# Layer norm of the spatial-gating branch: ordered behind an eviction on ScalarE instead of behind VectorE's last traced instruction

## The chip, the cores and the metric

The kernel runs on one core of a Trainium2 chip. The core has five engines that each work through a queue of their own: TensorE (PE) multiplies matrices, VectorE (DVE) and ScalarE (ACT) work on tiles elementwise, GpSimd (POOL) does simple elementwise work beside them, and SyncE (SP) issues the transfers here. They wait for each other through semaphores. The metric is the device time of one execution in microseconds, as the median of several runs. A profile of one execution shows every instruction with start, duration and the wait ahead of it.

## The reference

One layer of an encoder, on 2048 prompt frames and on 8 x 16 sample frames, with width 1024. What matters here:

```python
h = rmsnorm(x)
u, v, za, q, k, vv, zb, qi, ki, wi, ga, gb = split(h @ w_in)
# mixer A, spatial gating over chunks of 128 frames
u, v = gelu(u), gelu(v)
vn = (v - mean(v)) * rsqrt(var(v) + eps) * ln_g + ln_b          # the layer norm of this case
a = u * (masked sgu_w @ vn + sgu_b) * silu(za)
# mixer B, sparse attention
score = sum over heads of relu(qi . ki) * wi                    # masked by chunk
keep the 256 best keys of each row, softmax attention over them, times silu(zb)
# merge
y = x + (sigmoid(ga) * (a @ w_pa) + sigmoid(gb) * (b @ w_pb)) @ w_out, then rmsnorm
```

The normalised `vn` of the sample frames is an output as well.

## The kernel before

**Tiles and passes.** The frames are 17 tiles of 128 rows: 16 of the prompt and one (number 16) of all sample frames. They are worked on in two halves, `HALVES`: nine tiles (0 to 8) and eight (9 to 16). Projections are made in near-float32 precision with three matmuls each (`mm3`, L173): operands are split into a high part (`split_hi`, ScalarE, L179) and a low part (`split_lo`, L182).

**Phases.** `phase_p1` projects keys, values and queries, for half 0 and then for half 1. `phase_p2` does mixer A and the gates, for half 1 first ("the first pass" below, eight tiles) and then for half 0 ("the second pass", nine tiles). `phase_b` is the attention, tile by tile, with the attention of the sample frames (`attend_sample`, L899 and after) and early merges woven in. `phase_c` merges and projects out.

**Inside phase_p2**, for its tiles: project V in two blocks of 256 columns, evict from PSUM through a gelu on ScalarE into `vn` (L347). VectorE takes mean and variance of each tile (`stats`, L387 and L388), and the reciprocal root for all tiles (`rsqrt`, L186 to L190, into `rs`). Then block b = 0 of U is projected, two tiles to an eviction (L347 into `ug`); while that is traced, the generator `normal` is advanced two steps for each tile, so that the norm of a tile is traced beside U's projection. The norm is two instructions on VectorE in place: L395 subtracts the mean and multiplies by ln_g, L399 multiplies by the reciprocal root and adds ln_b. At its end, in the first pass, one transfer stores the sample tile's rows (L403). Then the first block of ZB is projected (evicted at L352 into "ev", two buffers), then four groups of spatial gating: a matmul of `sgu_w` with `vn` (L430; L435 for the sample tile) into a "tr" bank, and L432 on VectorE that multiplies it into `ug`. Then ZA is projected, evicted through silu into "ev" (L442) and multiplied into `ug` on GpSimd (L444); then the second block of ZB, then `ug` is transposed (L456) and stored; then all of it for block b = 1, and the gates (L472, L506). Projections use four PSUM banks ("mm"), transposes and spatial gating two ("tr"), scores two ("ix").

**The background.** Beside p1 of half 1 and all of p2 runs the selection of the 256 best keys (`select`), as two lanes. A tile's selection first needs scores (L535 and L536 on TensorE, L538 on ScalarE, L540 and L542 on VectorE), then 31 rounds of counting how many scores exceed a candidate (L612 on VectorE and L622 on ScalarE in turn, with small steps L623 to L628), then a mask that is stored (L654 to L663). The lanes take tiles 3, 5, 7, 9, 11, 13, 15 and 2, 4, 6, 8, 10, 16, 12, 14. `weave` mixes both streams into one program by estimated costs at a rate of 0.95.

**What sets the order.** The program order is not the order of the queues. Behind the tracing stands a planner, which plays the program against estimated durations and gives each engine, whenever it is free, the earliest traced instruction whose inputs are ready. An ordering edge without synchronisation makes an instruction stand behind another one in the planner's order; it emits no semaphore. `behind()` lays such an edge from each instruction of the norm to the VectorE instruction that was traced last before it, which by the weaving is often one of the selection.

Of the kernel before, what the change touches and what calls it, by code (L numbers as in the profile page):

```python
# [13 lines left out]
AF = mybir.ActivationFunctionType  # L14
OP = mybir.AluOpType
# [42 lines left out]
def encoder_step(ctx: ExitStack, tc: tile.TileContext, x_prompt, x_sample, cache_k, cache_v, cache_kidx,  # L58
                 norm_g, w_in, ln_g, ln_b, sgu_w, sgu_b, w_pa, w_pb, w_out, final_g,
                 y_prompt, y_sample, o_k, o_v, o_ki, s_k, s_v, s_ki, s_vn):  # L60
    nc = tc.nc
# [255 lines left out]

    AT_FROM = 1

    def behind():  # L320

        return tc.issue_after(next(i for i in reversed(nc.cur_bb.bb.instructions) if i.engine == mybir.EngineType.DVE))

    def phase_p2(half, hT, at_gates=None):

# [7 lines left out]
        def pairs(c, b, use, beside=None, of_beside=1):  # L333
            w = load_w([cols(c + 256 * b)])
            for i in range(0, nt, 2):
# [6 lines left out]
                            next(beside, None)  # L342
                use(pm[:, :m * 256].rearrange("p (j c) -> p j c", j=m), i, m, b * 256)

        def gelu_to(dst, at):
            def use(pm, i, m, c0):
                nc.scalar.activation(dst[:, i:i + m, at:at + 256], pm, AF.Gelu_apprx_tanh)  # L347
            return use

        def gate_b(pm, i, m, c0):  # L350
# [5 lines left out]
        lgb = p2.tile([P, 2, 512], F32, name="lgb")  # L356
# [21 lines left out]
        vn = p2.tile([P, nt, 512], F32, name="vn")  # L378
        st = p2.tile([P, 16, 6], F32, name="st")
        mv = p2.tile([P, 16, 2], F32, name="mv")  # L380
        rs = p2.tile([P, 3, 16], F32, name="rs")
# [9 lines left out]
        def normal():  # L391

            for i in range(nt):
                with behind():
                    nc.vector.scalar_tensor_tensor(vn[:, i], vn[:, i], mv[:, i, 0:1], lgb[:, 0],  # L395
                                                   op0=OP.subtract, op1=OP.mult)
                yield
                with behind():
                    nc.vector.scalar_tensor_tensor(vn[:, i], vn[:, i], rs[:, 1, i:i + 1], lgb[:, 1],  # L399
                                                   op0=OP.mult, op1=OP.add)  # L400
                yield
            if half:
                PS.dma_start(s_vn[0].rearrange("b s c -> (b s) c"), vn[:, nt - 1])  # L403

        beside = stats()
        for b in range(2):
            yield from pairs(C_V, b, gelu_to(vn, b * 256), beside if b else None)
# [3 lines left out]
        nc.vector.tensor_scalar(rs[:, 2, :nt], mv[:, :nt, 1], LN_EPS, None, op0=OP.add)  # L411
        rsqrt(rs[:, 1, :nt], rs[:, 0, :nt], rs[:, 2, :nt])
        beside = normal()
        at_s = {}
        for b in range(2):
            ug = p2.tile([P, nt, 256], F32, tag="ug", name="ug")
            yield from pairs(C_U, b, gelu_to(ug, 0), beside, 2)
            if b == 0:
                for _ in beside:
                    pass  # L420
                yield from pairs(C_ZB, 0, gate_b)
            for g in range(4):
# [3 lines left out]
                for i0 in range(0, np_, 8):  # L426
                    m = min(8, np_ - i0)
                    pm = bank("tr")
# [4 lines left out]
                if half:  # L433
                    pm = bank("tr")
# [14 lines left out]
            for gid, g in zip(gids, gs):  # L449
                i0 = tiles.index(g[0])  # L450
                m = len(g)
# [45 lines left out]
        for r in range(KD):  # L497
            w = load_w([cols(C_GA + P * r, P), w_pa[0][:, P * r:P * (r + 1)]])
            for gid in gids:
# [3 lines left out]
                pm = bank("mm")  # L503
# [609 lines left out]
    def at_gates():  # L1113
        px.append(Pool("p1c", side="right"))
        px.append(Normed(0, px[0], 2).ahead(2))

    back = weave(phase_p2(1, hT, at_gates), back, 0.95)
    hT = px[1].turn()
    px[0].close()
    back = weave(phase_p2(0, hT), back, 0.95)  # L1120
    wp.close()
    hp.close()
# [58 lines left out]
```

## Time and profile before

| | us |
|---|---|
| median of 3 runs | 2271.55 |
| lowest to highest | 2270.2 to 2272.07 |
| the profiled execution | 2267.2 |
| its span, first to last instruction | 2265.4 |
| TensorE busy | 2155.2 (95%) |
| VectorE busy | 1584.4 (70%) |
| ScalarE busy | 1217.8 (54%) |
| GpSimd busy | 592.2 (26%) |
| the norms of the first pass (first start to last start) | 455.5 to 492.1 |
| the norms of the second pass | 1052.8 to 1089.4 |

All times inside the run are microseconds from the start of the span. A row of the stretches gives start and end, length, then for each engine its busy time and how many instructions, then the clock granted to TensorE, the share of the transfer engines that was busy, and GB/s. A row of waits gives who waited for whom: microseconds in total, how often, the longest. A row of the chain of waits gives start, length, engine, and how many instructions in a row. PEld is the weight load of TensorE, which runs beside its matmuls.

### The profile page before, as it was taken

To read this page: it belongs to the slowest core of one execution; us is meant where nothing else is said; L and a number is where in the kernel's file an instruction comes from. 1 tells how busy PE (TensorE), PEld (TensorE's weight loads), DVE (VectorE), ACT (ScalarE), POOL (GpSimd) and SP (SyncE) were. 2 spreads that over 40 slices of the span, in tenths; PEclk is the share of its full clock that TensorE was granted. 3 is DMA by queue.
4 is the path that set the end of the run, shared out by engine and by line. 5 is a ranking of instruction groups with operands and counts; after the bars stand their busy time and mean duration, and the time that the engine had idled before them with its cause. 6 is when DMAs were issued, how large, how long until landed. Compare 5 with 4: busy or idle time off the path is not lost.

```text
span 2265.4 us, 38226 instructions
## 1 busy us (share of the span) xinstructions
PE 2155.2 (95%) x13896; PEld 2027.9 (90%) x13896; DVE 1584.4 (70%) x4057; ACT 1217.8 (54%) x2181; POOL 592.2 (26%) x693
## 2 busy tenths in 40 slices
PE   8999999999999999995799999989999999998998
PEld 7999999999999988993699999978889899987887
DVE  7105867897787797748996787577867689855442
ACT  6225546646665655435655654277756667753221
POOL 1221222232432231210125222123253423334100
PEclk9999999999999999995799999989999999999999
DMA  6233233122432233111115222454344431044342
GB/s 206 80 108 113 80 98 98 56 78 80 133 99 86 84 92 112 49 56 28 36 44 152 68 78 85 114 145 116 93 137 125 123 102 38 15 144 150 130 154 79
DMA packets 251005, 218.83 MB, mean 97 GB/s; under 512 B 46528, under 2 KB 238656, under 8 KB 250816
## 3 DMA queue, kind: packets, MB, share of 16 engines
q1 hardware_dynamic: 250816, 216.39, 32.3%
q8 instruction: 109, 1.79, 0.3%
q14 instruction: 80, 0.66, 0.1%
HBM read 152.45 MB, written 63.81 MB: 95 GB/s over the span
## 4 chain that ended last, share of the span: by engine, by line
PE 79%; DVE 7%; DMA 6%; ACT 3%; issue 2%; POOL 2%; SPq 1%; ACTq 0%; POOLq 0%; DVEq 0%
PE ps_mm L173 54%; PE ps_po L778 5%; PE ps_tr L761 4%; PE ps_ix L535 2%; PE ps_ix L536 2%; PE ps_mm L737 2%; PE ps_mm L738 2%; PE ps_ix L173 2%; DVE junk L612 2%; DMA ws<-in_w_in_dram 1%; PE ps_mm L789 1%; DMA qi<-qi_s 1%; DMA q<-q_s 1%; PE ps_tr L252 1%; POOL wl L182 1%
## 5 line engine op out<-in xcount | busy, mean ns | idle before, releaser
L182 POOL TENSOR_TENSOR wl<-ws,wh 128x256 fp32r<-128x256 f32 (+1 forms) x376 | 306.2, 844 | 930.1 <-ACT wh L179 895.3
L173 PE MATMUL ps_mm<-wh,hh 128*128 128x256 f32 (+1 forms) x1360 | 395.7, 292 | 5.7 <-ACT hh L179 3.5
L622 ACT ACTIVATE junk<-s,bc 128x384 int8<-128x384 f32 (+14 forms) x232 | 294.1, 1268 | 196.7 <-DVE bc L628 195.4
L173 PE MATMUL ps_mm<-wh,hl 128*128 128x256 f32 (+1 forms) x1360 | 395.3, 291 | 0.9 <-DVE hl L182 0.9
L173 PE MATMUL ps_mm<-wl,hh 128*128 128x256 f32 (+1 forms) x1360 | 393.9, 290 | 0.2 <-POOL wl L182 0.2
L173 PE MATMUL ps_mm<-hh,wh 128*128 128x384 f32 (+1 forms) x1152 | 378.2, 328 | 0.0
L173 PE MATMUL ps_mm<-hl,wh 128*128 128x384 f32 (+1 forms) x1152 | 377.7, 328 | 0.0
L173 PE MATMUL ps_mm<-hh,wl 128*128 128x384 f32 (+1 forms) x1152 | 376.8, 328 | 0.0
L612 DVE TENSOR_SCALAR_CACHE_REDUCE junk<-s,bc 128x512 int8<-128x512 f32 (+14 forms) x248 | 351.7, 1421 | 5.0
L173 PEld LDWEIGHTS ps_mm<-wh,hh 128*128 128x128 f32 x1360 | 262.2, 193 | 11.6 <-ACT hh L179 4.7
L173 PEld LDWEIGHTS ps_mm<-wh,hl 128*128 128x128 f32 x1360 | 262.2, 193 | 4.0 <-DVE hl L182 1.2
L173 PEld LDWEIGHTS ps_mm<-wl,hh 128*128 128x128 f32 x1360 | 262.3, 193 | 3.3 <-issue 1.2
L542 DVE SCALAR_TENSOR_TENSOR s<-r,wiw,s 128x384 f32<-128x384 f32 (+2 forms) x266 | 201.7, 780 | 65.3 <-ACT r L538 64.7
L173 PEld LDWEIGHTS ps_mm<-hh,wh 128*128 128x128 f32 x1152 | 217.1, 188 | 2.2
L173 PEld LDWEIGHTS ps_mm<-hl,wh 128*128 128x128 f32 x1152 | 217.1, 189 | 1.6
L173 PEld LDWEIGHTS ps_mm<-hh,wl 128*128 128x128 f32 x1152 | 217.0, 188 | 1.8
L538 ACT ACTIVATE r<-ps_ix 128x512 f32<-128x512 f32 (+2 forms) x304 | 156.7, 538 | 100.0 <-PE ps_ix L536 89.9
L761 PE MATMUL ps_tr<-ident,sx 128*128 128x128 f32 x1088 | 169.6, 275 | 5.3 <-DVE ptl L182 4.2
L182 DVE TENSOR_TENSOR ptl<-ps_tr,pth 128x512 fp32r<-128x512 f32 (+1 forms) x231 | 149.9, 659 | 28.4 <-ACT pth L179 27.2
L744 ACT ACTIVATE sx<-sx,mx 128x128 f32<-128x128 f32 (+15 forms) x128 | 153.7, 1202 | 29.0 <-DVE mx L743 28.5
L179 ACT ACTIVATE pth<-ps_tr 128x512 fp32r<-128x512 f32 (+1 forms) x231 | 126.9, 572 | 64.9 <-PE ps_tr L761 57.3
L778 PE MATMUL ps_po<-pth,vst 128*128 128x256 f32 x544 | 157.1, 306 | 3.3 <-ACT pth L179 1.8
(287 smaller groups left out, 4578.5 us busy)
## 6 DMA issues: line engine op xcount, KB each, us to landing
ws<-in_w_in_dram SPq DMA_DIRECT2D x88, 512.0 KB, 3.9
x<-in_x_prompt_dram SPq DMA_DIRECT2D x41, 512.0 KB, 3.6
q<-q_s SPq DMA_DIRECT2D x34, 256.0 KB, 4.1
out_dram<-x SPq DMA_DIRECT2D x17, 512.0 KB, 2.6
gb_s<-ev SPq DMA_DIRECT2D x40, 192.0 KB, 2.3
ma_s<-ev SPq DMA_DIRECT2D x40, 192.0 KB, 1.9
ma<-ma_s SPq DMA_DIRECT2D x40, 192.0 KB, 3.1
sg<-gb_s SPq DMA_DIRECT2D x40, 192.0 KB, 2.5
```

The source lines that it names most:

```text
L173: nc.tensor.matmul(out, a(k), b(k), start=(n == 0), stop=(n == 3 * nk - 1))
L179: nc.scalar.activation(dst, src, AF.Copy)
L182: (eng or nc.vector).tensor_tensor(dst, src, hi.bitcast(F32), op=OP.subtract)
L535: nc.tensor.matmul(pi[:, :n], hi[:, h, :], kist[:, c:c + n], start=True, stop=False)
L536: nc.tensor.matmul(pi[:, :n], lo[:, h, :], kist[:, c:c + n], start=False, stop=True)
L538: nc.scalar.activation(r[:, :n], pi[:, :n], AF.Relu, scale=HD ** -0.5)
L542: nc.vector.scalar_tensor_tensor(s[:, c:c + n], r[:, :n], wiw[:, t, h:h + 1], s[:, c:c + n], op0=OP.mult, op1=OP.add)
L612: nc.vector.tensor_scalar(junk[:, :L], s[:, :L], thr, 0.0, op0=op, op1=OP.add, accum_out=cnt)
L622: nc.scalar.activation(junk[:, :L], s[:, :L], AF.Sign, bias=candf, scale=-1.0, accum_out=cnt)
L744: nc.scalar.activation(sx, sx, AF.Exp, bias=mx[:, 7:8], scale=HD ** -0.5, accum_out=T.rsum[:, h:h + 1])
L761: nc.tensor.transpose(tv[:, l, hh * P:(hh + 1) * P], pr[hh][:, (l0 + l) * P:(l0 + l + 1) * P], ident)
L778: nc.tensor.matmul(po, vst[:, l0 + l, n, :], pp[:, l, :], start=(l0 + l == 0 and i == 0), stop=(l0 + l == t and i == 1))
```

## The change

`behind()` goes away. In its place `issue_behind(ins, before)` lays one ordering edge without synchronisation from an instruction to another one, also of another engine. The gelu eviction of V and U keeps its instruction in `evicted[0]`. The first step of a tile's norm (L395) is laid behind the gelu eviction that was traced last, so behind V's last one for tiles 0 and 1 of the pass, behind U's first for tiles 2 and 3, and so on, two tiles to an eviction. The second step (L399) has no ordering edge any more; it needs the first by its data.

```diff
-    def behind():
-
-        return tc.issue_after(next(i for i in reversed(nc.cur_bb.bb.instructions) if i.engine == mybir.EngineType.DVE))
+    def issue_behind(ins, before):
+
+        tc.add_manual_dep(ins.ins, before.ins.name,
+                          mybir.DependencyInfo(mybir.DependencyClass.NoSync, mybir.DependencyReason.DATA),
+                          reason="issue_behind")
...
+        evicted = [None]
+
         def gelu_to(dst, at):
             def use(pm, i, m, c0):
-                nc.scalar.activation(dst[:, i:i + m, at:at + 256], pm, AF.Gelu_apprx_tanh)
+                evicted[0] = nc.scalar.activation(dst[:, i:i + m, at:at + 256], pm, AF.Gelu_apprx_tanh)
             return use
...
             for i in range(nt):
-                with behind():
-                    nc.vector.scalar_tensor_tensor(vn[:, i], vn[:, i], mv[:, i, 0:1], lgb[:, 0],
-                                                   op0=OP.subtract, op1=OP.mult)
+                issue_behind(nc.vector.scalar_tensor_tensor(vn[:, i], vn[:, i], mv[:, i, 0:1], lgb[:, 0],
+                                                            op0=OP.subtract, op1=OP.mult), evicted[0])
                 yield
-                with behind():
-                    nc.vector.scalar_tensor_tensor(vn[:, i], vn[:, i], rs[:, 1, i:i + 1], lgb[:, 1],
-                                                   op0=OP.mult, op1=OP.add)
+                nc.vector.scalar_tensor_tensor(vn[:, i], vn[:, i], rs[:, 1, i:i + 1], lgb[:, 1],
+                                               op0=OP.mult, op1=OP.add)
                 yield
```

## The prediction

> **What bounds the kernel now.** I read the page first: the forty slices and the chain of waits.
>
> ```profile
> PE   8999999999999999995799999989999999998998
> ...
> PEclk9999999999999999995799999989999999999999
> ...
> PE 79%; DVE 7%; DMA 6%; ACT 3%; issue 2%; POOL 2%; SPq 1%; ACTq 0%; POOLq 0%; DVEq 0%
> ```
>
> TensorE sets the time nearly everywhere. The exception is slices 19 and 20 of 40 (56.6 us each, so 1019 to 1133 us), where PE falls to 5 and 7 tenths and its clock with it. Idle and slow PE time there is what can be won. Next, busy time by stretch: the hole, the stretch behind it, the start of the attention phase.
>
> ```profile
> core 0: us, PE busy (x) PEld busy (x) DVE busy (x) ACT busy (x) POOL busy (x), PEclk, DMA share, GB/s
> 930.00:955.00 25.00, 25.00 (x211) 25.00 (x210) 14.24 (x62) 12.24 (x26) 5.65 (x8) 1.00 0.17 49
> 1017.00:1103.00 86.00, 45.61 (x102) 24.05 (x101) 74.72 (x153) 44.77 (x67) 6.87 (x9) 0.56 0.09 24
> 1103.00:1465.00 362.00, 361.72 (x2213) 354.85 (x2213) 276.57 (x529) 194.42 (x282) 101.63 (x123) 0.99 0.29 85
> 1465.00:1505.00 40.00, 32.27 (x160) 26.22 (x161) 25.86 (x107) 27.66 (x83) 8.59 (x9) 0.74 0.69 169
> ```
>
> In 1017 to 1103, PE is idle 40.4 of 86 us and runs at a clock of 0.56; in the 362 us after, it is never idle. So whatever fills the hole moves all of 1103 to 1465 forward. Then, who waits for whom in the hole: first PE's waits, then all engines'.
>
> ```profile
> PE ps_tr L430 <- DVE vn L399: 17.0, 2, 15.0
> PE ps_ix L535 <- ACT qih L179: 11.7, 2, 5.9
> ...
> POOL ug L444 <- DVE bg L627: 75.8, 1, 75.8
> ```
>
> The spatial-gating matmuls (L430) wait for the second layer-norm step (L399). That looks like 17 us, but GpSimd's L444 has stood still 75.8 us: it multiplies the gate into ug, which L432 fills from L430's output. While it stands, by the code, the two "ev" buffers and then the "mm" banks stay taken, and no projection can be evicted. What PE does in the hole is scores for the background selection, and their small waits (L535) fill time in which PE has nothing else. The root is the norms' lateness. The two steps' busy time by stretch (L395; L399's row for the last stretch is the same), and the evictions of U and of the ZB projection after it (first and last start):
>
> ```profile
> 455.00:493.00 38.00, 5.98 (x8) 1.00 0.28 77
> 925.00:1050.00 125.00, 0.00 (x0) 0.91 0.17 50
> 1050.00:1092.00 42.00, 6.68 (x9) 0.50 0.05 13
> ...
> L347 ACT ACTIVATE ug<-ps_mm x5: 383/598/599, 931.3 to 950.4; 128x512 f32<-128x512 f32 x4, 128x256 f32<-128x256 f32 x1
> ...
> L352 ACT ACTIVATE ev<-ps_mm x5: 385/597/600, 956.8 to 977.0; 128x512 f32<-128x512 f32 x4, 128x256 f32<-128x256 f32 x1
> ```
>
> In the second pass the nine tiles are normalised between 1050 and 1092, though U's evictions were over at 951. The timeline of VectorE shows what they are queued behind:
>
> ```profile
> 932.10 0.17 DVE L190 TENSOR_TENSOR rs<-rs 128x9 f32<-128x9 f32 x1
> ...
> 1060.86 2.08 DVE L612 TENSOR_SCALAR_CACHE_REDUCE junk<-s,bc 128x1792 int8<-128x1792 f32 x1
> ...
> 1062.86 0.75 DVE L395 SCALAR_TENSOR_TENSOR vn<-vn,mv,lgb 128x512 f32<-128x512 f32 x1
> 1063.53 0.74 DVE L542 SCALAR_TENSOR_TENSOR s<-r,wiw,s 128x512 f32<-128x512 f32 x1
> ...
> 1086.13 2.08 PE L430 MATMUL ps_tr<-vn,wst 128*128 128x512 f32 x2 [15.00 <-DVE vn L399]
> ```
>
> Their last input (rs, L190) is complete at 932.3; they stand behind counts and scores of the selections of tiles 13 and 12 (1792 and 1664 columns), the work traced before them. The selection runs over 100 us behind its place in the program, and the edge carries that lag into the norms.
>
> **The change part by part.** It removes 34 ordering edges (17 tiles, two steps) on VectorE, and adds 17, from each first step to an eviction on ScalarE; a second step follows its first by its data alone. No instruction is added or dropped, and the new edge is order only, without a wait. If one were emitted after all, the evictions it names in the second pass lie at or before 947.5 (U's last but one), before or among the norms' possible places, and VectorE idles 10.8 of 25 us in 930 to 955; behind such a wait stand only selection steps, on which no projection depends. I take 0.
>
> *Second pass, the norms.* 18 instructions at 0.74 us (6.68 + 6.68 = 13.4 us in all) need that idle time: 10.8 us to 955 and the rest soon after, so vn is complete near 960 to 965, before the ZB projection, the next in the program, is through (its last eviction is at 977). L430 then runs without a wait.
>
> *The hole.* What PE must still do in 1017.5 to 1102.7 (85.2 us), by form, and the same at full clock from the chain of waits elsewhere:
>
> ```profile
> L535 PE MATMUL ps_ix<-kist,qih 128*128 128x384 f32 x26 | 14.8, 570 | 6.9 <-ACT r L538 6.6
> L536 PE MATMUL ps_ix<-kist,qi 128*128 128x384 f32 x26 | 12.8, 494 | 0.0
> L430 PE MATMUL ps_tr<-vn,wst 128*128 128x512 f32 x8 | 8.2, 1135 | 15.5 <-DVE vn L399 15.0 <-DVE ug L432 0.5
> L535 PE MATMUL ps_ix<-kist,qih 128*128 128x512 f32 x11 | 7.6, 709 | 14.1 <-ACT qih L179 11.7 <-ACT r L538 2.4
> L536 PE MATMUL ps_ix<-kist,qi 128*128 128x512 f32 x11 | 6.6, 616 | 0.2
> ...
> 974.11 0.23 PE ps_ix L535
> ...
> 1152.69 1.03 PE ps_tr L430 x4
> ...
> 1157.37 0.86 PE ps_tr L430 x2
> 1188.69 0.66 PE ps_tr L456 x6
> ```
>
> 22 score matmuls of 512 columns at 0.235 us are 5.2; 52 of 384 at three quarters of that, 9.2; eight large L430 at 0.43 are 3.4, eight small at (1.03 - 0.86) / 2 = 0.085 are 0.7; L456 with two projection matmuls, 0.9. Sum 19.4 us. The hole is worth at most 85.2 - 19.4 = **65.8 us**: the last gate matmul, now at 1465, would end near 1399.
>
> *What is late next.* The selection. Its last mask piece and, on the chain, PE's first step after the gates:
>
> ```profile
> L661 DVE SCALAR_TENSOR_TENSOR pen<-junk,eq x4: 550/687/692, 1442.6 to 1453.0; 128x512 bf16<-128x512 int8 x3, 128x384 bf16<-128x384 int8 x1
> ...
> 1465.20 0.44 PE ps_ix L899 x2
> ...
> 1400.00:1440.00 40.00, 40.00 (x231) 40.00 (x230) 25.94 (x54) 16.00 (x21) 8.53 (x12) 1.00 0.20 64
> ```
>
> It ends at 1453.0 + 0.55 = 1453.6, 12 us before the gates. VectorE is 87% busy in the hole (74.72 of 86), so the selection is paced by it there. Taking the norms' 13.4 us out brings its end to about 1440. Between 1399 and 1440 PE has the attention phase to start on. The selection leaves VectorE free for 35% (25.94 of 40 busy), and the attention phase used 65% of it (25.86 of 40), so I let it go at 0.35 / 0.65 = 54% of its pace: 41 x 0.54 = 22 us. Gain: 1465 - 1440 = 25, and 22 more, **47 us**. Bounds: nothing of the attention phase before the selection ends gives 25, no contention 66. I take 47, since the VectorE rows price the overlap.
>
> *Clock.* Two stretches of 10 us, columns as above. A PE 81% busy stayed at 0.50; at 100% it came back.
>
> ```profile
> 1050.00:1060.00 10.00, 8.08 (x18) 4.99 (x19) 9.93 (x20) 6.29 (x12) 0.00 (x0) 0.50 0.00 0
> 1110.00:1120.00 10.00, 10.00 (x87) 10.00 (x86) 9.62 (x25) 8.43 (x11) 0.00 (x0) 1.00 0.16 54
> ```
>
> In 1399 to 1440 PE would be 54% of 81% busy (32.27 of 40), so perhaps at half clock; its work there at full clock is 41 x 0.44 = 18 us, 36 at half, and still fits. So the sum stands. [...]
>
> *First pass.* The eight norms stand at 455 to 493, the U evictions are over at 441, so they move forward by some 35 us. PE was 37.4 of 40 us busy in the stretch of L430:
>
> ```profile
> L347 ACT ACTIVATE ug<-ps_mm x4: 592/597/599, 420.9 to 440.7; 128x512 f32<-128x512 f32 x4
> ...
> 480.00:520.00 40.00, 37.40 (x266) 34.86 (x265) 38.00 (x101) 18.45 (x34) 14.37 (x17) 0.91 0.21 66
> L403 SPq DMA_DIRECT2D out_dram<-vn x1: 357/357/357, 492.8 to 492.8; - x1
> ```
>
> At most 2.6 us of idle and 0.09 x 40 = 3.6 of clock come back; a loss of the same size is as possible, if norms displace selection steps on a VectorE that is 38 of 40 busy. I take 0 of -6 to +6. The one transfer moved is the store of the last tile (L403). It goes forward with the norms on SyncE's queue; a load behind it can only start earlier.
>
> *Sum.* The profiled execution took 2267.2 us, its span 2265.4. 2267.2 - 47 = 2220. The median of the runs, 2271.55, is 4.35 above the profiled one, so the forecast is **2224**. Its own range, 25 to 66 won and the first pass's 6 halved either way: 2202 to 2250.
>
> **Rivals.**
>
> *The selection gates everything behind it.* On PE, the first step behind the gates is L899 of the sample attention, which needs the selection's memory and came 11.6 us after the mask (1465.2). If the planner leaves L899 ahead of the attention phase in PE's queue, PE waits until 1440 + 12 = 1452: gain 13, **2258**. For it: that is today's order. Against: the tiles of the attention phase do not need that memory, and a planner that orders by readiness will see PE free.
>
> *Slower: the scores are thinned out.* In the hole PE gave the scores of tile 12 a pair every 1.4 us; where projections compete for PE, tiles 15 and 14 got one every 2.6.
>
> ```profile
> L535 PE MATMUL ps_ix<-kist,qih x62: 332/390/796, 1159.8 to 1321.4; 128*128 128x512 f32 x54, 128*128 128x384 f32 x8
> ...
> L535 PE MATMUL ps_ix<-kist,qih x37: 393/558/797, 1017.6 to 1069.2; 128*128 128x384 f32 x26, 128*128 128x512 f32 x11
> ```
>
> (161.6 / 62 and 51.6 / 37.) A filled hole makes the 32 pairs of tile 12 take 32 x 1.2 = 38 us more. If nothing of that is won back and L899 still stands first, PE restarts at 1453.6 + 38 + 11.6 = 1503: 38 us lost, **2310**. It decides once the mask's end comes after 1453.6. Against: the other lane counts faster meanwhile, and tiles 15 and 14 are scored only after it.
>
> *The change does not do what it says.* The planner still puts older VectorE work first, the norms stay at 1050: **2271**. Against: VectorE idled 43% of 930 to 955, with no older work ready.
>
> **Chances.** Forecast 0.59, PE held by the selection 0.20, no effect 0.08, slower 0.10, more than 66 won 0.03. A measurement here tells 0.2% (4.5 us) from no change. Faster: 0.59 + 0.20 + 0.03 = 0.82; same 0.08; slower 0.10. The range takes the forecast and the first rival: 2200 to 2264.
>
> **What would show it.** L395 and L399 of the second pass at 932 to 970; no wait of L430 for vn and none of L444 over 10 us; slices 19 and 20 of PE and clock at 9; the last gate matmul near 1400; the last L661 near 1440; attention matmuls (L737) before it. Wrong, if the norms are early and the hole stays (then something other than vn holds "ev"), or if PE idles as long just before L899.

## The result and the profile after

| | before | after |
|---|---|---|
| median of 4 runs each, same chip, us | 2270.88 | 2242.09 |
| lowest to highest | 2269.09 to 2272.07 | 2231.59 to 2244.56 |
| the profiled execution | 2267.2 | 2242.49 |

The ratio is 0.9865, with a 95% interval of 0.9833 to 0.9897: the changed kernel is faster by 28.8 us in the medians, 24.7 between the two profiled executions. The forecast was 2224, with 47 us gained. The hole was filled as forecast, all 66 us of it, but 41 us were given back in the attention phase.

The page after, its totals and three of the lines of its forty slices:

```profile
span 2240.7 us, 38226 instructions
...
PE 2144.5 (96%) x13896; PEld 2030.0 (91%) x13896; DVE 1588.7 (71%) x4057; ACT 1215.8 (54%) x2181; POOL 594.8 (27%) x693
...
PE   8999999999999999999999999588999999998998
...
DVE  7105857988897797856787678899788677755443
...
PEclk9999999999999999999999999699999999999999
```

The dip of PE and of its clock has left slices 19 and 20. A new one stands in slices 26 to 28 (a slice is now 56.0 us, so 1400 to 1568), where PE is at 5, 8 and 8 tenths and the clock at 6 in the first. It is shallower and longer. VectorE (DVE) is at 8, 9 and 9 there.

Line numbers have moved by two or three: the norm's steps are L398 and L401 (were L395 and L399), counting is L614 (was L612), the last step of a score L544 (was L542), a mask piece L663 (was L661), the gates L508 (was L506), attention logits L739 (was L737), the sample attention L901 (was L899). The norms of the second pass, the end of the gates, the last mask and the start of the attention, by source line:

```profile
L398 DVE SCALAR_TENSOR_TENSOR vn<-vn,mv,lgb x9: 717/745/1159, 919.0 to 943.8; 128x512 f32<-128x512 f32 x9
L401 DVE SCALAR_TENSOR_TENSOR vn<-vn,rs,lgb x9: 741/752/1229, 928.8 to 944.6; 128x512 f32<-128x512 f32 x9
L508 DVE TENSOR_TENSOR ev<-ev,ps_mm x15: 529/550/555, 1305.0 to 1398.8; 128x384 f32<-128x384 f32 x15
L663 DVE SCALAR_TENSOR_TENSOR pen<-junk,eq x8: 556/683/693, 1390.0 to 1555.6; 128x512 bf16<-128x512 int8 x7, 128x384 bf16<-128x384 int8 x1
L739 PE MATMUL ps_mm<-kst,qh x320: 280/403/668, 1411.2 to 1968.9; 128*128 128x512 f32 x92, 128*128 128x384 f32 x60, 128*128 128x128 f32 x4, 128*128 128x256 f32 x4
L901 PE MATMUL ps_ix<-ident,kc x32: 270/272/421, 1568.1 to 1713.7; 128*128 128x128 f32 x32
```

The same lines of the kernel before, where the prediction did not show them:

```profile
L506 DVE TENSOR_TENSOR ev<-ev,ps_mm x24: 528/550/555, 1320.5 to 1464.4; 128x384 f32<-128x384 f32 x24
L737 PE MATMUL ps_mm<-kst,qh x320: 278/396/776, 1475.9 to 1993.5; 128*128 128x512 f32 x92, 128*128 128x384 f32 x60, 128*128 128x128 f32 x4, 128*128 128x256 f32 x4
```

The norms are through at 945 (before: 1090). The last gate starts at 1398.8 instead of 1464.4, the attention at 1411.2 instead of 1475.9: both 65 us earlier. But the last mask piece starts at 1555.6, 103 us later than the 1453.0 of before, and the last attention logit is only 25 us earlier (1968.9 against 1993.5).

Where the 41 us went is read from the stretches, first of after (the old hole, the overlap of selection and attention in two cuts, the rest, the whole attention phase), then of before (the first 157 us of its attention phase and all of it). The columns are those of the prediction's stretches.

```profile
1017.00:1103.00 86.00, 85.26 (x649) 82.00 (x648) 61.16 (x112) 53.43 (x86) 19.12 (x22) 1.00 0.22 64
...
1399.00:1440.00 41.00, 21.76 (x93) 17.94 (x94) 32.19 (x106) 27.47 (x66) 7.74 (x8) 0.58 0.53 124
1399.00:1556.00 157.00, 115.89 (x706) 102.98 (x707) 140.31 (x422) 111.42 (x248) 42.80 (x43) 0.83 0.35 87
1556.00:1985.00 429.00, 421.90 (x2936) 389.70 (x2935) 329.65 (x926) 292.31 (x518) 149.56 (x160) 0.99 0.36 97
1399.00:1985.00 586.00, 537.80 (x3639) 492.69 (x3640) 469.96 (x1347) 403.74 (x765) 192.35 (x203) 0.94 0.35 95
```

```profile
1465.00:1622.00 157.00, 143.83 (x944) 125.99 (x944) 120.46 (x429) 120.05 (x302) 42.74 (x48) 0.93 0.46 118
1465.00:2010.00 545.00, 521.69 (x3636) 480.83 (x3636) 420.86 (x1246) 385.70 (x745) 186.36 (x194) 0.97 0.35 97
```

The old hole holds 85.26 us of PE work in 86, at full clock. The attention phase, with the same work (3639 matmuls in the trace, 3636 before), takes 586 us instead of 545. Of these 41 us, 25 are PE idle (586 - 537.8 = 48.2 against 545 - 521.7 = 23.3) and 16 are the same work at a lower clock (537.8 against 521.7 busy, clock 0.94 against 0.97). Both lie in the first 157 us, up to the end of the last mask: 706 matmuls are done there instead of 944. VectorE is 89% busy in it (140.31) against 77% (120.46). Counting alone (L614) is 27 us of that, in this row of the same stretch with only that line's instructions:

```profile
1399.00:1556.00 157.00, 26.59 (x24) 0.83 0.35 87
```

Gain and loss add up: 66 - 41 = 25, the difference of the profiled executions.

Why is the selection 103 us late? Tile 14 is the last one of its lane, behind tile 12. The scores of tile 12, by the accumulating step on VectorE of 28 of its 32 pairs, before and after:

```profile
L542 DVE SCALAR_TENSOR_TENSOR s<-r,wiw,s x28: 607/612/751, 1033.3 to 1066.6; 128x384 f32<-128x384 f32 x21, 128x512 f32<-128x512 f32 x7
```

```profile
L544 DVE SCALAR_TENSOR_TENSOR s<-r,wiw,s x28: 603/620/1257, 1049.5 to 1102.6; 128x384 f32<-128x384 f32 x21, 128x512 f32<-128x512 f32 x7
```

In the hole they took 33 us, among projections 53, and they end 36 us later. The counting of tile 14 follows, its first and last count on VectorE, before and after:

```profile
L612 DVE TENSOR_SCALAR_CACHE_REDUCE junk<-s x1: 2153/2153/2153, 1323.3 to 1323.3; 128x1920 int8<-128x1920 f32 x1
...
L612 DVE TENSOR_SCALAR_CACHE_REDUCE junk<-s,bc x24: 2187/2212/2347, 1303.0 to 1437.4; 128x1920 int8<-128x1920 f32 x17, 128x2048 int8<-128x2048 f32 x7
```

```profile
L614 DVE TENSOR_SCALAR_CACHE_REDUCE junk<-s x1: 2153/2153/2153, 1351.0 to 1351.0; 128x1920 int8<-128x1920 f32 x1
...
L614 DVE TENSOR_SCALAR_CACHE_REDUCE junk<-s,bc x23: 2197/2212/2347, 1339.7 to 1512.7; 128x1920 int8<-128x1920 f32 x17, 128x2048 int8<-128x2048 f32 x6
```

It starts 28 us late (1351.0 against 1323.3), takes 162 us instead of 114, and its last mask piece starts 43 us after the last count instead of 16: 28 + 48 + 27 gives the 103. Before, this tail lay under the gates, and the two together left VectorE 35% free (25.94 of 40 us busy from 1400 to 1440); now most of it (1399 to 1556) lies under the attention, which kept VectorE 77% busy without it (120.46 of 157 in the kernel before). The tail also holds up a part of the attention: `attend_sample` begins by freeing the memory of the selection, and its first matmul (L901) starts at 1568.1, 12.5 us after the last mask piece; with the tail shortened, in the second run below, it starts at 1479.1, 14 us after that run's last piece. Of the 238 matmuls that are missing in the first 157 us, 147 are those of the sample attention (before, 147 stand in 1465 to 1622; after, none in 1399 to 1556), and 91 are those of the tiles (797 before, 706 after).

### The profile page after: what moved, and what is told of

Its sections match the earlier page's. It is cut to its first block, busy times and chain, and to the rows that moved or that the text cites. A ratio compares the mean times of both kernels' runs of the same rounds, so it can differ in the third digit from the quotient of the medians.

```text
span 2240.7 us, 38226 instructions
## 1 busy us (share of the span) xinstructions
PE 2144.5 (96%) x13896; PEld 2030.0 (91%) x13896; DVE 1588.7 (71%) x4057; ACT 1215.8 (54%) x2181; POOL 594.8 (27%) x693
## 5 line engine op out<-in xcount | busy, mean ns | idle before, releaser
L182 POOL TENSOR_TENSOR wl<-ws,wh 128x256 fp32r<-128x256 f32 (+1 forms) x376 | 310.7, 856 | 915.7 <-ACT wh L179 903.7
L614 DVE TENSOR_SCALAR_CACHE_REDUCE junk<-s,bc 128x512 int8<-128x512 f32 (+14 forms) x248 | 351.9, 1421 | 5.2
L544 DVE SCALAR_TENSOR_TENSOR s<-r,wiw,s 128x384 f32<-128x384 f32 (+2 forms) x266 | 201.5, 774 | 65.0 <-ACT r L540 64.2
L763 PE MATMUL ps_tr<-ident,sx 128*128 128x128 f32 x1088 | 177.0, 281 | 14.8 <-ACT sx L746 4.3
L780 PE MATMUL ps_po<-pth,vst 128*128 128x256 f32 x544 | 161.7, 313 | 9.3 <-ACT osb L784 8.8
L182 DVE TENSOR_TENSOR ptl<-ps_tr,pth 128x512 fp32r<-128x512 f32 (+1 forms) x231 | 149.6, 658 | 28.7 <-ACT pth L179 27.7
```

The source lines that it names most:

```text
L182: (eng or nc.vector).tensor_tensor(dst, src, hi.bitcast(F32), op=OP.subtract)
L544: nc.vector.scalar_tensor_tensor(s[:, c:c + n], r[:, :n], wiw[:, t, h:h + 1], s[:, c:c + n], op0=OP.mult, op1=OP.add)
L614: nc.vector.tensor_scalar(junk[:, :L], s[:, :L], thr, 0.0, op0=op, op1=OP.add, accum_out=cnt)
L763: nc.tensor.transpose(tv[:, l, hh * P:(hh + 1) * P], pr[hh][:, (l0 + l) * P:(l0 + l + 1) * P], ident)
L780: nc.tensor.matmul(po, vst[:, l0 + l, n, :], pp[:, l, :], start=(l0 + l == 0 and i == 0), stop=(l0 + l == t and i == 1))
```

## The experiments

All were timed against the kernel before on the same chip. Its median was 2268.11 to 2270.01 in these sets, against 2270.88 in the table above, so distances between kernels of different sets can be off by up to 3 us. Two theories were tested first, called A and B in what was expected. By A, the 41 us are the price of the selection's tail sharing VectorE with the attention. By B, the attention phase loses them whether the tail is there or not.

**The tail shortened, without and with the change.** In both kernels tile 14 counts 10 of its 31 rounds; the other 21 are left out, so its threshold is coarse.

```diff
-        for b in range(30, -1, -1):
+        for b in range(30, 20 if t == 14 else -1, -1):
```

> The kernel before, where the selection of tile 14, the last to finish, counts 10 of its 31 rounds; 21 rounds are left out, so its mask is not exact. Control for the next run. Theory A (66 us were won before the gates' end, and 41 of them are given back because the selection's tail runs into the attention phase on VectorE): here the tail ends before the gates anyway, so the time hardly moves, 2262 to 2271 us, gates still end near 1465. Theory B (the attention phase has a slow start of its own whenever it begins, for its loads and the half clock): the same, 2262 to 2271.

> The changed kernel with the same 21 rounds of tile 14 left out. Theory A: the selection ends near 1400, the gates near 1399, so the whole 66 us stays: 2200 to 2212 us, 55 us or more under the run above, PE idle and half clock behind the gates as in the kernel before (attention phase 545 us long). Theory B: the start stays slow, 2230 to 2242 us, 28 us under the run above, attention phase 586 us long.

Measured: 2266.56 on the kernel before (ratio 0.9984, 0.9973 to 0.9996), 2219.99 on the changed one (0.9774, 0.9752 to 0.9796). The tail is worth almost nothing before and 22 us after, so it is part of the give-back; but 2220 lies between the two theories. VectorE's timeline of the shortened changed kernel shows that the tail had not gone:

```profile
1404.26 0.74 DVE L661 SCALAR_TENSOR_TENSOR eq<-pre,bd,eq 128x512 f32<-128x512 f32 x1
...
1457.25 1.28 DVE L657 TENSOR_TENSOR_SCAN pre<-eq,bl 128x512 f32<-128x512 f32 x1
1458.56 0.67 DVE L741 CUSTOM_DVE_ANT_0 sx<-ps_mm,pen 128x512 f32<-128x512 f32 x1
1460.17 0.69 DVE L182 TENSOR_TENSOR ptl<-ps_tr,pth 128x512 fp32r<-128x512 f32 x1 [0.86 <-ACT pth L179]
...
1464.65 0.68 DVE L663 SCALAR_TENSOR_TENSOR pen<-junk,eq 128x512 bf16<-128x512 int8 x1
```

Masks (L657, L661, L663) still run among attention steps (L741 and the split L182) until 1465. So the test was made again with the tail gone.

**The tail taken away.** Tile 15 counts 10 rounds and tile 14 four; 48 rounds of the two are left out.

```diff
-        for b in range(30, -1, -1):
+        for b in range(30, {14: 26, 15: 20}.get(t, -1), -1):
```

> The kernel before with 10 rounds of tile 15 and 4 of tile 14 (the other 48 rounds left out): the selection ends near 1370, well before the gates, which stay near 1465. Both theories: 2255 to 2268 us. Control for the next run.

> The changed kernel with the same rounds left out, so that the masks too are done before 1400 (in the earlier run with 10 rounds of tile 14 two masks, 8 pieces, still ran to 1465 in the attention phase, and 47 of 66 us were kept). Theory A, the tail of the selection on VectorE is the whole of what is given back: 60 to 67 us under the run above. Theory B, part of the loss belongs to the attention phase itself: the distance stays at 45 to 52 us.

Measured: 2264.25 before (0.9981, 0.9968 to 0.9993) and 2200.15 after (0.97, 0.9684 to 0.9716). Without the tail the change is worth 64.1 us, the size of the hole. Masks and attention of the changed kernel without the tail:

```profile
L663 DVE SCALAR_TENSOR_TENSOR pen<-junk,eq x12: 283/692/1225, 1221.0 to 1383.0; 128x512 bf16<-128x512 int8 x10, 128x128 bf16<-128x128 int8 x1, 128x384 bf16<-128x384 int8 x1
...
1396.00:1553.00 157.00, 144.07 (x945) 125.82 (x945) 120.64 (x430) 119.63 (x302) 41.57 (x48) 0.95 0.47 117
1396.00:1941.00 545.00, 522.22 (x3634) 480.05 (x3634) 420.81 (x1247) 385.56 (x745) 185.46 (x194) 0.98 0.35 97
...
L901 PE MATMUL ps_ix<-ident,kc x32: 270/273/435, 1395.6 to 1536.7; 128*128 128x128 f32 x32
```

The last mask starts before the attention does, and the attention phase is the old one again, 545 us with 522 us of PE work. B falls, and of A it is shown that the tail is the whole of what is given back. How the tail costs that is not shown: without it VectorE is less busy (120.64 of 157 us), but the sample attention also starts with the attention phase again (L901 at 1395.6), and this test does not separate the two, nor VectorE's time from ScalarE's or from that of small transfers. PE's longest waits in the overlap of the changed kernel (1399 to 1556) name no single engine either:

```profile
PE ps_tr L699 <- DMA kk<-out_dram: 11.5, 2, 7.1
PE ps_po L780 <- ACT osb L784: 7.7, 5, 2.6
PE ps_mm L739 <- DVE mx L741: 6.2, 3, 3.6
```

**VectorE relieved in the overlap.** One of five splits of the attention's probabilities goes over GpSimd; here three of five for the tiles 0 to 5.

```diff
-            if turn[0] % POOL_OF in POOL_TURNS:
+            if turn[0] % POOL_OF in (POOL_TURNS if t > 5 else (0, 2, 4)):
```

> The changed kernel, where for attention tiles 0 to 5 three of five splits of the probabilities go to GpSimd instead of one of five: some 19 splits of 0.66 us, 12 us, leave VectorE in the stretch where it is busy 152.6 of 170 us (1390 to 1560). Theory A (VectorE bounds that stretch): 4 to 12 us faster than the changed kernel, 2230 to 2238 us, and the selection's last mask earlier than 1556. Rival (latency and ScalarE, which gets one more copy a split, bound it): 2242 us or more.

Measured: 2231.01 (0.9836, 0.9817 to 0.9855), 11 us under the full change by the medians; the two intervals overlap (0.9833 to 0.9897 for the full change), so the gain is not clear of the spread. The overlap:

```profile
1399.00:1556.00 157.00, 121.87 (x735) 106.48 (x736) 138.21 (x424) 116.78 (x260) 80.91 (x91) 0.83 0.45 113
...
L663 DVE SCALAR_TENSOR_TENSOR pen<-junk,eq x6: 540/690/1110, 1399.9 to 1526.1; 128x512 bf16<-128x512 int8 x5, 128x384 bf16<-128x384 int8 x1
```

GpSimd takes 38 us more, the last mask starts 30 us earlier (1526.1), and PE does 6 us more in the stretch, where it is still 35 us idle. So VectorE's load holds the tail up. How much it holds the attention up is not shown: of the 29 matmuls more, 19 are those of the sample attention, which starts earlier too (1537.5), and up to 1526, with the tail in both kernels, 552 are done against 537.

**The second pass alone.** The old edges stay in the first pass.

```diff
...
+            if half:
+                for i in range(nt):
+                    with behind():
...
+            else:
+                for i in range(nt):
+                    issue_behind(...)
...
```

> The new edge in the second pass alone, the old edges in the first. Theory A and B: all of the gain comes from the hole of the second pass: 2239 to 2246 us, the same as the full change within 4 us. Rival C (the first pass has a share, by moving the later order): over 2250 or under 2235 us.

Measured: 2239.71 (0.9874, 0.9851 to 0.9897), as the full change. The norms by pass:

```profile
L404 DVE SCALAR_TENSOR_TENSOR vn<-vn,mv,lgb x8: 743/747/748, 453.4 to 488.5; 128x512 f32<-128x512 f32 x8
...
L413 DVE SCALAR_TENSOR_TENSOR vn<-vn,mv,lgb x9: 734/743/750, 921.7 to 946.2; 128x512 f32<-128x512 f32 x9
```

The first pass keeps its old places (453 to 489) and nothing is missing: the gain comes from the second pass.

**No ordering edge at all.**

```diff
-                issue_behind(nc.vector.scalar_tensor_tensor(...), evicted[0])
+                nc.vector.scalar_tensor_tensor(...)
```

> The changed kernel without the new edge: the norms have no ordering edge at all. Theory: what helps is that the old edge is gone, the evictions named by the new one are over before a norm's turn comes; 2238 to 2247 us, the norms of the second pass at 915 to 950 as in the changed kernel. Rival (the new edge holds the norms back from displacing statistics or selection steps): over 2250 us.

Measured: 2228.65 (0.9825, 0.9804 to 0.9846), 13 us under the changed kernel by the medians and outside what was expected; the ends of the two intervals overlap. Norms, and a stretch of the second pass without the edge, then that stretch with it:

```profile
L398 DVE SCALAR_TENSOR_TENSOR vn<-vn,mv,lgb x9: 714/747/1294, 897.7 to 922.3; 128x512 f32<-128x512 f32 x9
...
1110.00:1200.00 90.00, 89.36 (x508) 87.89 (x507) 74.98 (x150) 59.99 (x94) 34.25 (x40) 1.00 0.41 128
```

```profile
1110.00:1200.00 90.00, 87.09 (x488) 85.33 (x487) 73.51 (x151) 60.24 (x93) 33.75 (x37) 0.98 0.38 117
```

The norms start 21 us earlier still (897.7 against 919.0), so the new edge does hold them back, against the theory. PE idles 2 us less in this stretch, and the gates end about 10 us earlier. A single wait that went away was not found; the whole order changes a little. What this gain is stays open; in the last run below it does not show.

**A third bank for the scores.** The selection is late because tile 12's scores are slow. By the prediction that was TensorE's share; a score also waits for one of two banks to be evicted (before, from 1010 to 1110, the score matmuls L535 waited ten times for the eviction L538, 8.9 us in all). One bank of the projections is given to it, on the changed kernel and on the kernel before.

```diff
-    bank.set(mm=4, tr=2, ix=2)
+    bank.set(mm=3, tr=2, ix=3)
```

> The changed kernel with three PSUM banks for scores and three for projections, instead of two and four. Theory (scores are thinned out because a pair waits for a bank while projections take PE in turn): the scores of tile 12 take under 55 us instead of some 62 (1043 to 1105), tile 14's counting starts before 1340 instead of 1351, and the time is 2228 to 2240 us. Rival (three banks hold the projections up as much): 2242 to 2260 us.

> The kernel before, with its old edges, and three PSUM banks for scores and three for projections. The old edge holds a norm until the selection reaches the place traced ahead of it; with three banks tile 13 was counted from 956 instead of 1029 us in the changed kernel, so the selection's lag shrinks by some 73 us. Theory (the hole is the selection's lag, carried into the norms by the old edge): the norms come near 980 to 1015, the hole shrinks from 85 us to 15 or less, 2205 to 2225 us. Rival (the hole belongs to the edge whatever the lag): the hole stays, 2240 us or more, only the tail is freed.

Measured: 2202.43 on the changed kernel (0.9708, 0.9693 to 0.9722), far below what was expected, and the fastest kernel of this study that leaves no rounds out, 40 us under the changed one and 68 under the one before. On the kernel before, 2210.66 (0.9743, 0.9724 to 0.9761), 57 us won by the banks alone. The changed kernel with three banks: its scores of tile 12, its last mask and gates, and its stretches.

```profile
L544 DVE SCALAR_TENSOR_TENSOR s<-r,wiw,s x28: 603/614/1220, 967.7 to 1001.3; 128x384 f32<-128x384 f32 x21, 128x512 f32<-128x512 f32 x7
...
L663 DVE SCALAR_TENSOR_TENSOR pen<-junk,eq x8: 559/692/1111, 1280.9 to 1350.7; 128x512 bf16<-128x512 int8 x7, 128x384 bf16<-128x384 int8 x1
L508 DVE TENSOR_TENSOR ev<-ev,ps_mm x17: 542/553/556, 1303.3 to 1401.1; 128x384 f32<-128x384 f32 x17
...
960.00:1060.00 100.00, 100.00 (x785) 97.31 (x784) 87.54 (x192) 72.35 (x104) 25.05 (x33) 1.00 0.20 60
1402.00:1559.00 157.00, 146.00 (x931) 126.25 (x931) 118.63 (x424) 117.95 (x297) 40.18 (x46) 0.91 0.45 115
```

With PE 100% busy the 28 pairs take 33.6 us, as long as with two banks and an idle PE (33.3). The last mask starts at 1350.7, before the gates end, and the overlap is gone: PE does 146.00 us of work in the first 157 us of the attention, as before the change (143.83). The gates end 2 us later (1401.6 against 1399.3), so the projections lose little that shows. The edit also takes a bank from the projections, and the 28 pairs now stand some 80 us earlier; which of these makes the pairs faster was not tested apart. The kernel before with three banks, its norms and the same stretch:

```profile
L395 DVE SCALAR_TENSOR_TENSOR vn<-vn,mv,lgb x9: 740/745/1320, 989.5 to 1026.0; 128x512 f32<-128x512 f32 x9
...
960.00:1060.00 100.00, 94.40 (x698) 89.52 (x697) 86.80 (x180) 66.37 (x94) 24.01 (x33) 0.95 0.17 51
```

The old edges stand, but the selection that they carry runs ahead, so the norms come at 990 and only 5.6 us of PE are left idle. The hole was the old edge times the selection's lag; with three banks the change of this case is worth 8 us (2210.66 against 2202.43).

**No edge, three banks.** Both edits together.

> The norms without any ordering edge, and three score banks: the two versions that were fastest by themselves (2228.65 and 2202.43 us). If what the missing edge won (13 us) is its own: 2188 to 2196 us. If it was won only against the selection's lag, which the third bank has taken away: 2198 to 2207 us.

Measured: 2207.25 (0.9726, 0.9702 to 0.9751), not better than 2202.43. What the missing edge won with two banks, if it was clear of the spread, is not its own.

## Why the prediction was right or wrong

*What bounds the kernel, and the root of the hole: right.* With the norms early, the spatial gating's wait for vn has gone. PE's longest wait from 900 to 1399 after the change:

```profile
PE ps_mm L173 <- ACT ev L474: 2.4, 1, 2.4
```

GpSimd's multiply (now L446) did wait 14.8 us once, where the prediction had none over 10; it was for ScalarE, not for vn, and PE did not stand behind it, as its longest wait, 2.4 us, shows. GpSimd's row in the same stretch:

```profile
POOL ug L446 <- ACT r L540: 14.8, 1, 14.8
```

*The norms of the second pass: right* (919 to 945, predicted 932 to 970). What the new edge costs is not settled: without any edge the norms start 21 us earlier and the median is 13 us lower, but with three banks it is not lower.

*The hole: right.* 65.8 us at most were worked out, 65 to 66 measured. *First pass: right*, 0 of -6 to +6: the first norm moved forward by 43 us (412.5 from 455.5; some 35 forecast), and the second pass alone gives the same time.

*What is late next: this step failed.* "Taking the norms' 13.4 us out brings its end to about 1440." It came to 1556, later than before instead of earlier. The step kept the pace that the selection has while PE is empty, and took only VectorE's relief into account. But the hole was also what fed it: in it the scores had PE to themselves. The prediction saw this in its slower rival, with 38 us for tile 12, and put the 38 us into that rival alone, where they belonged in the sum of the forecast as well. (Measured: 36 us later, 20 of them by slower scores, 53 against 33 us for 28 pairs, and 16 by a later start, so the good agreement is partly luck.) Only 28 of the 103 us were there when the counting of tile 14 began. The other 75 came while the tail ran beside the gates and the attention; the forecast let the attention go slower beside the selection, but not the selection beside the attention.

*The pace of the overlap: near in the stretch that was priced, but not its cause.* The 54% was taken for 41 us. From 1399 to 1440, 93 matmuls were done, about as many as the kernel before did in its first 25 us of attention:

```profile
1465.00:1490.00 25.00, 20.38 (x88) 16.04 (x89) 13.37 (x65) 14.63 (x43) 2.47 (x3) 0.66 0.80 199
```

By this count some 15 us were lost there, with 41 - 22 = 19 forecast. But the overlap lasted 157 us, and over all of it the attention lost 41, so it ran at 74% of its pace (1 - 41 / 157). At 54% an overlap of that length would have cost 72 us, more than the hole was worth, and the change would have lost. The overlap was far longer than forecast and its later part cheaper; these two partly cancelled, so that the time came within the forecast's own range is partly luck. And the price was derived from VectorE's free time, while more than half of the missing matmuls (147 of 238) are the sample attention's, which waited for the selection's memory.

*Clock.* That PE would run near half clock in 1399 to 1440 was right (0.58). That it costs nothing was wrong: the low clock lasted beyond 1440, and over the attention phase it took 16 of the 41 us. The stretches behind 1430:

```profile
1430.00:1440.00 10.00, 7.58 (x39) 6.22 (x39) 7.73 (x26) 9.47 (x28) 3.62 (x4) 0.70 0.47 113
1440.00:1450.00 10.00, 7.45 (x39) 7.24 (x37) 8.27 (x25) 6.84 (x19) 3.17 (x4) 0.66 0.27 74
...
1460.00:1470.00 10.00, 8.48 (x59) 7.04 (x58) 9.61 (x30) 6.61 (x20) 5.20 (x6) 1.00 0.32 93
1470.00:1480.00 10.00, 7.82 (x55) 6.71 (x56) 9.71 (x33) 10.00 (x22) 3.18 (x4) 1.00 0.53 126
```

A PE that was 85% and 78% busy ran at 1.00. So the busy share of a stretch does not tell the clock, and the step from one stretch at 81% and 0.50 to a forecast of half clock was the author's estimate. Before, PE stood idle for 5.95 us (1021.00 to 1026.95); the clock was at 1.00 up to 1023 and at 0.50 from 1024 to 1033. From 1460 to 1480 after the change, PE's longest idle time was 1.95 us, with the clock at 1.00. What decides when the clock falls, and when it comes back, is not shown.

*The rivals.* PE held by the selection (2258): half of it came. The sample attention did wait for the selection (L901 at 1568.1), but it did not stand first in PE's queue, and PE worked on the tiles of the prompt meanwhile, idle for 41 of 157 us. Slower, by thinned-out scores (2310): its mechanism is the start of the 41 us, for it gave the first 28 of the 103 us by which the selection ended later; its condition, the sample attention first on PE, was not met. No effect: wrong.

## What to carry to other kernels

An ordering edge behind "whatever was traced last" on an engine carries the backlog of any stream that is woven in there (here the norms started 120 us behind their last input, at 1052.8 against 932.3); look for that stream's lag, not only for the edge. A stall on the bounding engine can feed a background stream (here 28 pairs of scores took 33 us in the hole and 53 without it): before counting a filled stall as gain, work out when that stream will end without it, and what it then shares an engine with, or keeps waiting for its memory. If a stream of small, dependent steps is late, try its buffer depth first: here one more bank for the scores, taken from the projections, was worth more than the edge (57 us against 29).

## What was not expected of the hardware

With three banks for the scores and three for the projections, 28 pairs of scores took 33.6 us beside a PE that was 100% busy, as long as with two banks in a PE that had little else (33.3 us; 53 us with two banks among projections), and the gates ended 2 us later (1401.6 against 1399.3). TensorE's clock was at 1.00 with PE 78% busy over 10 us (1470 to 1480 after the change), where it had stayed at 0.50 with PE 81% busy (1050 to 1060 before); what decides between them was not settled.
